# Writing down TensorE's order in the RWKV layer of a four-layer trunk

## The chip, the core and the metric

The kernel runs as one program on one core of a Trainium2 chip. The metric is the device time of one execution in microseconds (us). The engines are named as the profile names them: PE is TensorE (PEld its weight loads), DVE is VectorE, ACT is ScalarE, POOL is GpSimd, SP issues DMAs. Each engine works through its own queue in the order in which the compiled program put it there.

## The reference

A sequence of 1024 tokens and a context of 256 tokens, 1024 wide, go through four mixer layers: 0 and 3 are gated linear recurrences, 1 is an mLSTM, and layer 2 is the RWKV-7 mixer that this case is about. Cut to what matters, layer 2 is

```
xs = h + (shifted - h) * mu                     # six mixtures of h and its shift
r, k, v, z = xs[:4] @ w_rkvz                    # four projections, 1024 x 1024 each
decay, a = low-rank functions of xs[4], xs[5]
for t, forward and then again backward, per head of 64:
    s = s * decay_t - (s @ kk_t) (kk_t * a_t)^T + v_t k_t^T
    y_t = s @ r_t
out = (groupnorm(y) + bonus) * silu(z) @ w_out
x = x + gate * out
```

The context is scanned first, and its last states start the scan of the sequence, in both directions. All is float32 at the borders.

## The kernel before, in words

The 1280 tokens are five blocks of 256, the channels eight tiles `e` of 128 (two heads each). `rwkv_scan` does layer 2. Two kinds of work share the engines in it.

**The scan** runs in 40 batches. `batch(n)` gives a step `i` (0 to 4) and a tile `e`; tiles 0 to 3 run in batches 0 to 19, tiles 4 to 7 in batches 20 to 39. One batch is one block forward and one block backward of one tile, in four chunks of 64 tokens. It has four functions:
- `prep(n)` makes the chunk operands. For each direction two small matmuls (pA below: L1043, L1045) give decay and rate, ACT and DVE turn them into `AR` and `BK`, then sixteen matmuls of `AR` with `BK` (L1093, two halves of eight, pB below) fill PSUM banks `px`; ACT copies parts of them into `DG` (L1098, L1099), of which there is one buffer, and `RB`, and DVE masks the rest into `X` (L1102). Transposes of `BK` follow (L1111).
- `inverse(n)` inverts the triangular 64 x 64 blocks. DVE transposes `DG` into `LN` (L1147), does a forward substitution of 28 small instructions (L1164, L1165), transposes back (L1167) and transposes the 16 x 16 inverses into `E16` (L1171). Then TensorE doubles the block size twice, in four groups of 32 x 32 matmuls (L1177, L1182, L1189, L1195; i1 to i4 below), with ACT copies and DVE additions between them (L1184, L1185).
- `chain(n, step)` is one chunk of the recurrence: matmuls c1 (L1236), an ACT copy, c2 (L1240), ACT copies, c3 (L1246), four DVE updates of the state in `UZ` or `st`, and the output matmuls c4 (L1253, L1255).
- `finish(n)` is the group norm of a batch whose two directions are summed.

The loop over `n` issues, in this order: steps 2 and 3 of batch n-1 interleaved with steps 0 and 1 of batch n, `finish(n - 2)`, `inverse(n + 1)`, `prep(n + 2)`, and then projections.

**The projections** are the generators `group` and `output`. One pass is `project`: eight input tiles `xs`, eight times the three matmuls of `mm3` (L110 to L112; each float32 operand is a high and a low part) into a bank of `pz`, after which ACT or DVE empties the bank. `mixed` makes one input tile (ACT L861, DVE L81, ACT L881, POOL L86), `half` one half of a pass's weights (DMA, ACT L890, POOL L86), `kk_norm` normalizes a tile of keys with two more small matmuls (L982, L990). The value projection (L924 to L926) has tokens as the stationary operand. The list `fill` says in which batches which generator is pulled, and how often: 8 pulls in batches 0 to 1, 14 in 2 to 5, 10 in 6 to 9, 12 in 10 to 17, 12 in 18 to 25, 24 in 26 to 30, 24 in 31 to 36, 8 in 38 to 40.

What sets the order: the program is traced in the order above, and a scheduler then orders each engine's queue by its own model of the machine, with the trace's order as priority. `issue_after` keeps DVE's part of the projections of batch n behind the last DVE instruction of batch n-3. So the order in which projections and scan share TensorE is the scheduler's, not the source's.

Of the kernel before, what the change touches and what calls it, by code (L numbers as in the profile page):

```python
# [11 lines left out]
ALU = mybir.AluOpType  # L12
# [16 lines left out]
class Net:  # L29
# [756 lines left out]
    def rwkv_scan(self, es, hd, zd, yd, xd):  # L786
# [107 lines left out]
        def project(w_ap, xs, n):  # L894
            ps = bank(pz, "pz")[:, 0:n]
            for k in range(len(xs)):
                if k % 4 == 0:
                    w = half(w_ap[:, k * 128:k * 128 + 512])
                self.mm3(ps, w, k % 4, xs[k], (0, n), k == 0, k == len(xs) - 1)
            return ps  # L900

# [3 lines left out]

        def group(blks, what, wave=0):
            n = 256 * len(blks)
            for g in what:
                xs = [mixed(g, k, blks) for k in range(8)]
                if g >= 4:  # L910
                    ps = project(self.a["r7_l1"][g - 4], xs, n)
                    t = tile_("po", [128, 512], bufs=3)
                    S.activation(out=t[:, 0:n], in_=ps, func=AF.Tanh if g == 4 else AF.Copy)
                    out_blocks(blks, lambda b: ld[b][:, g - 4, :], t)
                    yield
                elif g == 2:
                    for i, b in enumerate(blks):
                        for q in (wave,):
                            acc = [bank(pz, "pz") for _ in range(2)]
                            for k in range(8):  # L920
                                w = half(self.a["r7_wv"][q][:, k * 512:k * 512 + 512])
                                for c in range(2):
                                    tk = slice(i * 256 + c * 128, i * 256 + c * 128 + 128)
                                    mm(acc[c], xs[k][0][:, tk], w[0], start=k == 0, stop=False)  # L924
                                    mm(acc[c], xs[k][0][:, tk], w[1], start=False, stop=False)
                                    mm(acc[c], xs[k][1][:, tk], w[0], start=False, stop=k == 7)  # L926
                                if k == 3:
                                    yield
                            for c in range(2):
                                t = tile_("po", [128, 512], bufs=3)  # L930
                                S.copy(out=t, in_=acc[c])
                                for j in (0, 1):
                                    nc.sync.dma_start(out=vd[b][8 * q:8 * q + 8, :, 2 * c + j, :].rearrange("h s v -> s h v"),
                                                      in_=t[hr[j]].rearrange("p (h v) -> p h v", h=8))
                            yield
                else:
                    for e in range(4 * wave, 4 * wave + 4):
                        ps = project(self.a["r7_w"][g, e], xs, n)
                        t = tile_("po", [128, 512], bufs=3)
                        if g == 3:  # L940
                            S.activation(out=t[:, 0:n], in_=ps, func=AF.Tanh, scale=0.5)
                            self.stt(V, t[:, 0:n], t[:, 0:n], 1.0, ps, ALU.add, ALU.mult)
                            out_blocks(blks, lambda b: zd[e][:, b * 256:(b + 1) * 256], t)
                        else:
                            S.copy(out=t[:, 0:n], in_=ps)
                            out_blocks(blks, lambda b: krk[b][e, :, 1 - g, :], t)
                        if g == 1:
                            kk_norm(e, t, n, blks)
                        yield

        def output(blks, ks, src):

            n = 256 * len(blks)
            xs = []
            for k in ks:
# [8 lines left out]
                xs.append((hi, lo))  # L964
            s = 0 if blks[0] else 1
            for e in range(8):
                t = tile_("po", [128, 512], bufs=3)
                for i, b in enumerate(blks):
                    nc.sync.dma_start(out=t[:, i * 256:(i + 1) * 256], in_=src[e][:, b * 256:(b + 1) * 256])
                ps = project(self.a["r7_w_out"][e][:, ks[0] * 128:], xs, n)  # L970
                self.stt(V, t[:, 0:n], ps, gate[:, e, s:s + 1], t[:, 0:n], ALU.mult, ALU.add)
                out_blocks(blks, lambda b: xd[e][:, b * 256:(b + 1) * 256], t)
                yield

        def kk_norm(e, kt, n, blks):

            sq = tile_("kq", [128, 512], bufs=1)
            S.activation(out=sq[:, 0:n], in_=kt[:, 0:n], func=AF.Square, scale=kk_v[:, e:e + 1])
            nt = n // 128
            ps = bank(pi, "pi")  # L980
# [7 lines left out]
            ps = bank(pi, "pi")  # L988
# [27 lines left out]
        def prep(n):  # L1016
# [16 lines left out]
            for d in (0, 1):  # L1033
# [10 lines left out]
                for o, w, j in oj:  # L1044
                    mm(o, w[r], lw[1][r, j, :], start=False, stop=j == 1)  # L1045
                sg = sgs[d]
# [30 lines left out]
                X = tile_("X%d" % d, [128, 4, 2, 128], bufs=3)  # L1077
# [224 lines left out]
        def run(*gens):  # L1302
            for g in gens:
                yield from g
# [207 lines left out]
```

## Time and profile before

| | us |
|---|---|
| median of 3 runs (4715.73 to 4727.37) | 4717.35 |
| the profiled execution's own time | 4715.13 |
| its span, first to last instruction | 4713.0 |
| PE busy, whole span (87%) | 4093.5 |
| DVE busy, whole span (70%) | 3313.9 |
| ACT busy, whole span (45%) | 2110.1 |
| POOL busy, whole span (48%) | 2271.5 |

The scan of layer 2 fills the span from about 2030 to about 4100 us. Busy is the share of time in which the engine ran at least one instruction. [...] "Idle before" in a group's row is the time that the engine stood still just before such an instruction, with what ended it.

### The profile page before, as it was taken

The numbers are of one execution on the slowest core, as the hardware profiler recorded it, in microseconds if no ns is written. First come the engines' busy times: TensorE is split into PE (matmuls) and PEld (weight loads), VectorE is DVE, ScalarE is ACT, GpSimd is POOL, SyncE is SP. The second block draws the span as 40 slices with busy tenths as digits, with TensorE's granted clock in tenths as the row PEclk, the third lists the DMA queues.
The fourth block names the chain that finished last, engine by engine and source line by source line (L and its number), as shares of the span: only waits on it lengthen the run. The fifth ranks groups of instructions, "written<-read, shape, count | busy, mean of one in ns | idle before, by whom it ended". The sixth has DMA issues, their size and how long they took to land. (4 is left out here: it accounts for less than half of the span.)

```text
span 4713.0 us, 84318 instructions
## 1 busy us (share of the span) xinstructions
PE 4093.5 (87%) x32068; PEld 3313.0 (70%) x32068; DVE 3313.9 (70%) x6218; ACT 2110.1 (45%) x4476; POOL 2271.5 (48%) x1989
## 2 busy tenths in 40 slices
PE   6999888999999989668988888888898888779988
PEld 3687768988889868445667666666666676557767
DVE  4478656545545533687988888988889889658875
ACT  3576322222222210645656545445566434256661
POOL 2466533333333331366666545555456654356662
PEclk9999989999999999768788777667588787689989
DMA  5311422222222342434444333223244443321122
GB/s 202 116 51 51 141 90 77 90 88 92 88 88 88 116 136 71 157 119 131 139 134 142 121 102 109 88 91 106 85 139 129 148 154 114 100 99 52 47 95 97
DMA packets 317749, 504.50 MB, mean 107 GB/s; under 512 B 55168, under 2 KB 201600, under 8 KB 317216
## 3 DMA queue, kind: packets, MB, share of 16 engines
q1 hardware_dynamic: 317344, 499.12, 33.1%
q8 instruction: 252, 4.13, 0.4%
q14 instruction: 153, 1.25, 0.1%
HBM read 406.02 MB, written 92.96 MB: 106 GB/s over the span
## 5 line engine op out<-in xcount | busy, mean ns | idle before, releaser
L86 POOL TENSOR_TENSOR wlo<-wraw,whi 128x512 fp32r<-128x512 f32 (+3 forms) x437 | 713.8, 1635 | 922.5 <-DVE whi L101 453.3
L112 PE MATMUL pm<-hhi,wlo 128*128 128x512 f32 (+1 forms) x1648 | 611.9, 374 | 32.1 <-POOL wlo L86 32.1
L111 PE MATMUL pm<-hlo,whi 128*128 128x512 f32 (+1 forms) x1648 | 620.1, 377 | 9.9 <-DVE hlo L81 9.9
L110 PE MATMUL pm<-hhi,whi 128*128 128x512 f32 (+1 forms) x1648 | 617.7, 375 | 0.6 <-ACT hhi L288 0.6
L101 DVE CAST whi<-wraw 128x1024 fp32r<-128x1024 f32 (+4 forms) x189 | 170.0, 900 | 336.5 <-PE pm L111 171.1
L86 POOL TENSOR_TENSOR xl<-mx,xh 128x512 fp32r<-128x512 f32 (+1 forms) x240 | 288.6, 1205 | 221.1 <-ACT xh L881 181.7
L110 PE MATMUL pz<-xh,whi 128*128 128x512 f32 (+1 forms) x784 | 333.8, 428 | 51.2 <-ACT whi L890 22.0
L112 PEld LDWEIGHTS pm<-hhi,wlo 128*128 128x128 f32 x1648 | 316.0, 192 | 87.2 <-POOL wlo L86 37.8
L111 PEld LDWEIGHTS pm<-hlo,whi 128*128 128x128 f32 x1648 | 316.0, 192 | 65.8 <-DVE hlo L81 11.4
L110 PEld LDWEIGHTS pm<-hhi,whi 128*128 128x128 f32 x1648 | 316.8, 192 | 53.8 <-issue 1.7
L111 PE MATMUL pz<-xl,whi 128*128 128x512 f32 (+1 forms) x784 | 330.1, 422 | 22.1 <-POOL xl L86 18.2
L110 PE MATMUL pm<-yhi,whi 128*128 128x512 f32 (+1 forms) x816 | 303.9, 377 | 44.5 <-DVE x L81 16.2
L112 PE MATMUL pz<-xh,wlo 128*128 128x512 f32 (+1 forms) x784 | 329.5, 421 | 6.7 <-POOL wlo L86 4.9
L111 PE MATMUL pm<-ylo,whi 128*128 128x512 f32 (+1 forms) x816 | 304.7, 374 | 3.9 <-POOL ylo L86 3.3
L112 PE MATMUL pm<-yhi,wlo 128*128 128x512 f32 (+1 forms) x816 | 297.9, 372 | 1.6 <-POOL wlo L86 1.6
L81 DVE SCALAR_TENSOR_TENSOR x<-pm,mod,x 128x512 f32<-128x512 f32 (+1 forms) x208 | 136.6, 665 | 184.3 <-PE pm L112 168.2
L1093 PE MATMUL px<-AR,BK 64*128 64x128 f32 x1280 | 204.3, 362 | 67.1 <-ACT BK L1071 37.6
L110 PEld LDWEIGHTS pz<-xh,whi 128*128 128x128 f32 x784 | 175.5, 225 | 94.9 <-ACT xh L881 28.2
L1093 PEld LDWEIGHTS px<-AR,BK 64*128 64x128 f32 x1280 | 171.9, 253 | 93.4 <-ACT BK L1071 46.1
L890 ACT CAST whi<-wraw 128x512 fp32r<-128x512 f32 x276 | 169.7, 617 | 142.5 <-PE pz L111 47.6
L81 DVE SCALAR_TENSOR_TENSOR mx<-hp,vecs,mx 128x256 f32<-128x256 f32 (+3 forms) x280 | 198.4, 731 | 46.3 <-ACT mx L861 45.5
L1164 DVE TENSOR_TENSOR ltmp<-LN 128x28 f32<-128x28 f32 (+6 forms) x560 | 219.0, 391 | 12.1
(356 smaller groups left out, 11041.3 us busy)
## 6 DMA issues: line engine op xcount, KB each, us to landing
wraw<-in_r_w SPq DMA_DIRECT2D x144, 256.0 KB, 3.1
kin<-r7krk SPq DMA_DIRECT2D x72, 384.0 KB, 3.3
mw<-in_mod_w SPq DMA_DIRECT2D x48, 512.0 KB, 6.9
mw<-in_mod_w SPq DMA_DIRECT2D x96, 256.0 KB, 2.6
wraw<-in_lru_w_in SPq DMA_DIRECT2D x40, 512.0 KB, 3.6
hp<-r7h SPq DMA_DIRECT2D x160, 128.0 KB, 2.2
wraw<-in_r_wv SPq DMA_DIRECT2D x80, 256.0 KB, 3.1
UZ<-r7v SPq DMA_DIRECT2D x160, 128.0 KB, 2.9
```

The source lines that it names most:

```text
L81: i = eng.scalar_tensor_tensor(out=out, in0=in0, scalar=scalar, in1=in1, op0=op0, op1=op1, **k)
L86: eng.tensor_tensor(out=out, in0=a, in1=b, op=op)
L101: nc.vector.tensor_copy(out=hi, in_=raw)
L110: mm(out, w[0][:, c], x[0][:, a:a + b], start=first, stop=False)
L111: mm(out, w[0][:, c], x[1][:, a:a + b], start=False, stop=False)
L112: mm(out, w[1][:, c], x[0][:, a:a + b], start=False, stop=last)
L890: S.copy(out=hi, in_=raw)
L1093: mm(pss[hh][:, c * 128:(c + 1) * 128], BK[r, c, 64 - 64 * hh:192 - 64 * hh], AR[r, c, :], start=True, stop=True)
L1164: V.tensor_tensor(out=tv, in0=c, in1=x, op=ALU.mult)
```

## The change: an order on TensorE

1. `group` and `output` no longer issue anything; they list passes. `rows` is a pass as before, cut into units of three matmuls (`mm3`); `cols` is the value projection, cut into units of six. `stream` walks the passes unit by unit, loads each half of the weights one half ahead, and makes the next pass's input tiles one by one during the last pass that uses the present ones. `kk_norm` is cut in three, runs its matmuls after units 2 and 5 of the next pass, and takes a bank of `pz` instead of `pi`.
2. `prep`, `inverse`, `chain` and `finish` become generators that yield where TensorE waits for another engine.
3. The time of a batch is a grid of 40 parts. `at` gives each piece of the scan its part; between two pieces `project` issues as many units as `rate` says: the projections of batches 6 to 37 now come from one stream at a constant 1488/32 = 46.5 matmuls of 512 columns per batch; batches 0 to 1 have (336 - 72)/2 = 132, batches 2 to 5 have 84.
4. At the end every TensorE instruction from `mark` on gets a dependency on the one before it (it orders the queue and adds no wait), so TensorE's order is the one written. The other engines' orders are still the scheduler's.

Matmuls, casts, vector instructions and DMAs are the same in kind; DVE has 5948 instructions in both programs.

```diff
+        def rows(job, w_ap, done):
+            n, ks = job.n, len(job.tiles)
+            hs = [w_ap[:, k * 128:k * 128 + 512] for k in range(0, ks, 4)]
+            def steps():
+                ps = bank(pz, "pz")[:, 0:n]
+                for k in range(ks):
+                    yield lambda w: self.mm3(ps, w, k % 4, job.xs[k], (0, n), k == 0, k == ks - 1)
+                done(ps)
+            return job, hs, 4, steps, 3 * n / 512
+        def stream(passes):
...
+            for pi_, (job, h, per, steps, cost) in enumerate(passes):
+                nxt = passes[pi_ + 1][0] if pi_ + 1 < len(passes) else job
...
+                for k, step in enumerate(steps()):
+                    if k % per == 0:
+                        if k:
+                            ready.pop(0)
+                        if len(ready) < 2:
+                            ahead()
+                    step(ready[0])
+                    if late and k in (2, 5):
+                        next(late[0], None)
...
+                    if nxt is not job:
+                        nxt.make()
+                    yield cost
...
-            ps = bank(pi, "pi")
+            ps = bank(pz, "pz")
...
+        INV = (10, 26, 28, 31, 33, 35, 36)
...
+        def project(amount):
+            nonlocal debt
+            debt += amount
+            while debt > 0:
+                with self.tc.issue_after(order_after[-3]) if len(order_after) >= 3 else ExitStack():
+                    c = next(dense, None)
+                if c is None:
+                    break
+                debt -= c
+        preps = {0: prep(0), 1: prep(1)}
+        drain(preps[0])
+        project(36)
+        drain(inverse(0))
+        project(36)
...
         for n in range(41):
-            for step in (0, 1):
-                if n:
-                    chain(n - 1, step + 2)
-                if n < 40:
-                    chain(n, step)
-            if n > 1:
-                finish(n - 2)
-            if n < 39:
-                inverse(n + 1)
-            if n < 38:
-                prep(n + 2)
+            dense, a, z, total = next(f for f in fill if f[1] <= n < f[2])
+            rate = (total - 72 * (a == 0)) / (z - a) / 40
...
+            for c, step, t in ((n - 1, 2, 0), (n - 1, 3, 16), (n, 0, 10), (n, 1, 26)):
+                if 0 <= c < 40:
+                    gens.append(at(chain(c, step), (t, t + 4, t + 8, t + 12, t + 14)))
+            if n < 39:
+                gens.append(at(preps[n + 1], (1, 5, 9, 11, 12)))
+                gens.append(at(inverse(n + 1), INV))
+            if n < 38:
+                preps[n + 2] = at(prep(n + 2), (13, 17, 19))
             if n > 1:
+                gens.append(at(finish(n - 2), (3, 21, 23)))
+            t0 = 0
+            for t, _, g in sorted(events, key=lambda v: v[:2]):
+                if t > t0:
+                    project(rate * (t - t0))
+                    t0 = t
+                next(g, None)
+            project(rate * (40 - t0))
...
+        last = None
+        for i in nc.cur_bb.bb.instructions[mark:]:
+            if str(i.engine).split(".")[-1] == "PE":
+                if last is not None:
+                    self.tc.add_manual_dep(i, last.name, mybir.DependencyInfo(mybir.DependencyClass.NoSync, mybir.DependencyReason.DATA), reason="order")
+                last = i
```

The order on TensorE before, where the inverse of batch 15 begins: the two halves of pB (L1093) of the next batch stand ahead of i1 (L1177).

```order
L1236 MATMUL pc<-UZ,X_26512 64x64
L1093 MATMUL px<-AR,BK 128x128 x4
L1236 MATMUL pc<-UZ,X_26512 64x64
L1236 MATMUL pc<-UZ,X_26545 64x64
L1093 MATMUL px<-AR,BK 128x128 x4
L1240 MATMUL pc<-U_27265,DT_16453 64x64 x3
L1177 MATMUL pi<-E_26886,DO 32x32 x32
L1111 MATMUL px<-ident,BK 128x64 x8
```

So the next batch's `DG` could be filled while this batch's i1 still waited. The order on TensorE in the change, at i1 (now L1241) of a batch in the constant part of the stream; c4 is now L1325 and L1327, i2 L1247.

```order
L1241 MATMUL pi<-E_35147,DO 32x32 x32
L110 MATMUL pz<-xh,whi 128x512
L111 MATMUL pz<-xl,whi 128x512
L112 MATMUL pz<-xh,wlo 128x512
L1325 MATMUL pc<-UZ,X_33796 64x64 x2
L1325 MATMUL pc<-UZ,X_33871 64x64 x2
L1327 MATMUL pc<-UZ,RB_33799 64x64 x2
L1327 MATMUL pc<-UZ,RB_33874 64x64 x2
L1247 MATMUL pi<-D_35146,QQ 32x32 x32
```

A unit of the projections and a piece of the scan alternate. Further on in the same queue, 24 rows after that i2, both halves of the next batch's pB (now L1153) come, behind i1 to i4:

```order
L1305 MATMUL pc<-UZ,X_34432 64x64 x2
L1305 MATMUL pc<-UZ,X_34466 64x64 x2
L1153 MATMUL px<-AR,BK 128x128 x8
L110 MATMUL pz<-xh,whi 128x512
L111 MATMUL pz<-xl,whi 128x512
L112 MATMUL pz<-xh,wlo 128x512
L1310 MATMUL pc<-U_35586,DT_16451 64x64 x4
L1153 MATMUL px<-AR,BK 128x128 x8
```

In the change pB of the next batch stands behind i1 in every batch.

## Rows read from the trace of the kernel before

**Rows 1.** The page: granted clock by fortieths of the span, in tenths.

```profile
PEclk9999989999999999768788777667588787689989
```

**Rows 2.** Busy time by stretch; columns stand in the header row.

```profile
core 0: us, PE busy (x) PEld busy (x) DVE busy (x) ACT busy (x) POOL busy (x), PEclk, DMA share, GB/s
2500.00:4000.00 1500.00, 1270.94 (x15124) 1001.48 (x15122) 1307.54 (x2824) 774.24 (x2090) 826.47 (x888) 0.75 0.39 117
```

**Rows 3.** VectorE's groups, 2100 to 4100: busy, mean ns, idle before.

```profile
L1102 DVE TENSOR_TENSOR X<-px,mk 64x512 f32<-64x512 f32 x152 | 104.4, 687 | 55.2 <-ACT RB L1101 52.0
L81 DVE SCALAR_TENSOR_TENSOR UZ<-UZ,W,pc 64x64 f32<-64x64 f32 x480 | 133.4, 278 | 31.7 <-PE pc L1246 20.3 <-ACT DT L1200 0.3
```

**Rows 4.** TensorE's groups, same stretch.

```profile
L1236 PE MATMUL pc<-UZ,X 128*64 128x64 f32 x1272 | 143.2, 281 | 55.8 <-DVE UZ L81 50.4 <-DMA mx<-y 2.8 <-DVE y L1258 1.8
L1177 PE MATMUL pi<-E,DO 32*32 32x32 f32 x2560 | 40.0, 208 | 17.9 <-DVE E L1171 13.1 <-DVE kq L81 4.8
L110 PE MATMUL pz<-xh,whi 128*128 128x512 f32 (+1 forms) x680 | 289.5, 428 | 18.4 <-ACT xh L881 9.8 <-ACT whi L890 2.8 <-DVE po L81 2.6
```

**Rows 5.** Timeline, VectorE: the LN transposes of batches 0, 6, 38 (start, us).

```profile
2026.12 2.07 DVE L1147 STREAM_TRANSPOSE LN<-DG 128x1024 f32<-128x1024 f32 x1 [2.95 <-ACT DG L1099]
2407.01 1.99 DVE L1147 STREAM_TRANSPOSE LN<-DG 128x1024 f32<-128x1024 f32 x1
3990.75 1.99 DVE L1147 STREAM_TRANSPOSE LN<-DG 128x1024 f32<-128x1024 f32 x1 [0.62 <-ACT DG L1099]
```

**Rows 6.** Timeline, batch 15 to 16: E16, pB, i1, LN.

```profile
2918.48 0.43 DVE L1171 STREAM_TRANSPOSE E<-D 128x256 f32<-128x256 f32 x1
2922.79 1.16 PE L1093 MATMUL px<-AR,BK 64*128 64x128 f32 x8
2924.25 0.75 PE L1177 MATMUL pi<-E,DO 32*32 32x32 f32 x64
2925.05 2.04 DVE L1147 STREAM_TRANSPOSE LN<-DG 128x1024 f32<-128x1024 f32 x1
```

**Rows 7.** Timeline, batch 26 to 27: E16, pB, c4, i1, c4, i2, pB, LN.

```profile
3429.57 0.44 DVE L1171 STREAM_TRANSPOSE E<-D 128x256 f32<-128x256 f32 x1
3429.64 1.16 PE L1093 MATMUL px<-AR,BK 64*128 64x128 f32 x16
3431.66 0.45 PE L1255 MATMUL pc<-UZ,RB 64*64 64x64 f32 x8
3432.41 0.75 PE L1177 MATMUL pi<-E,DO 32*32 32x32 f32 x64
3439.62 0.69 PE L1255 MATMUL pc<-UZ,RB 64*64 64x64 f32 x8
3440.24 1.07 PE L1182 MATMUL pi<-D,QQ 32*32 32x32 f32 x64
3441.25 2.08 PE L1093 MATMUL px<-AR,BK 64*128 64x128 f32 x16
3445.38 2.12 DVE L1147 STREAM_TRANSPOSE LN<-DG 128x1024 f32<-128x1024 f32 x1
```

**Rows 8.** Timeline, TensorE: projections at clock 0.5 and at 1.0.

```profile
2245.93 0.63 PE L925 MATMUL pz<-wlo,xh 128*128 128x512 f32 x1
2246.35 0.63 PE L926 MATMUL pz<-whi,xl 128*128 128x512 f32 x1
2272.61 0.39 PE L111 MATMUL pz<-xl,whi 128*128 128x512 f32 x1
2272.84 0.39 PE L112 MATMUL pz<-xh,wlo 128*128 128x512 f32 x1
```

**Rows 9.** Projection tiles alone, two stretches: busy, count, clock of the stretch.

```profile
3300.00:3400.00 100.00, 10.63 (x31) 7.21 (x29) 0.00 (x0) 1.17 (x2) 0.52 0.30 89
3400.00:3500.00 100.00, 49.02 (x188) 34.95 (x189) 4.37 (x8) 3.90 (x8) 0.81 0.43 128
```

**Rows 10.** Timeline, TensorE: i1 of batch 0.

```profile
2124.25 0.75 PE L1177 MATMUL pi<-E,DO 32*32 32x32 f32 x64
```

More of the change, by code (lines that the diff above doesn't have):

```diff
@@ L892, in half @@
             return hi, lo
[L894 to L900, printed above, removed]
         def out_blocks(blks, dst, t):
@@ new lines, in cols, with steps, mms @@
+        def cols(job, i, w_ap, done):
+            def steps():
+                acc = [bank(pz, "pz") for _ in range(2)]
+                for k in range(8):
+                    def mms(w):
+                        for c in range(2):
+                            tk = slice(i * 256 + c * 128, i * 256 + c * 128 + 128)
+                            mm(acc[c], job.xs[k][0][:, tk], w[0], start=k == 0, stop=False)
+                            mm(acc[c], job.xs[k][0][:, tk], w[1], start=False, stop=False)
+                            mm(acc[c], job.xs[k][1][:, tk], w[0], start=False, stop=k == 7)
+                    yield mms
+                for c in range(2):
+                    done(c, acc[c])
+            return job, [w_ap[:, k * 512:k * 512 + 512] for k in range(8)], 1, steps, 6
@@ new lines, in stream, with ahead @@
+        def stream(passes):
+            passes = list(passes)
+            hs = [ap for _, h, *_ in passes for ap in h]
+            ready = []
+            nh = 0
+            def ahead():
+                nonlocal nh
+                if nh < len(hs):
+                    ready.append(half(hs[nh]))
+                    nh += 1
+            for pi_, (job, h, per, steps, cost) in enumerate(passes):
+                nxt = passes[pi_ + 1][0] if pi_ + 1 < len(passes) else job
+                while len(job.xs) < len(job.tiles):
+                    job.make()
+                if not ready:
+                    ahead()
[4 more added lines that the diff above has]
+                        if len(ready) < 2:
+                            ahead()
+                    step(ready[0])
+                    if late and k in (2, 5):
+                        next(late[0], None)
+                        if k == 5:
+                            late.pop()
+                    if nxt is not job:
+                        nxt.make()
+                    yield cost
+                ready.pop(0)
+            drain(*late)
@@ L908, in group, with done @@
             for g in what:
-                xs = [mixed(g, k, blks) for k in range(8)]
+                job = Job(blks, [lambda g=g, k=k: mixed(g, k, blks) for k in range(8)])
                 if g >= 4:
[L911 to L915, printed above, removed]
+                    def done(ps, g=g):
+                        t = tile_("po", [128, 512], bufs=3)
+                        S.activation(out=t[:, 0:n], in_=ps, func=AF.Tanh if g == 4 else AF.Copy)
+                        out_blocks(blks, lambda b: ld[b][:, g - 4, :], t)
+                    yield rows(job, self.a["r7_l1"][g - 4], done)
@@ L916, in group @@
                 elif g == 2:
                     for i, b in enumerate(blks):
[L918 to L935, printed above, removed]
@@ L1298, in finish, with drain @@
                     mm(ps[r, c * 64:(c + 1) * 64], y[r, c, :], self.ident[r, r], start=True, stop=True)
+            yield
             S.activation(out=yo[:, 0:64 * m], in_=ps[:, 0:64 * m], func=AF.Identity, scale=0.5, bias=hlb[:, e:e + 1])
             out_blocks(blks, lambda blk: yd[e][:, blk * 256:(blk + 1) * 256], yo)
-        def run(*gens):
+        def drain(*gens):
             for g in gens:
-                yield from g
-        def pull(it, n):
-            for _ in range(n):
-                if next(it, 0) == 0:
-                    return
+                for _ in g:
+                    pass
         early = True
@@ L1384, in rwkv_scan @@
-        finish(39)
+        both = lambda *gens: (p for g in gens for p in g)
+        fill = [(stream(group(G1, (4, 5) + krv)), 0, 2, 336), (stream(group(G2, (4, 5) + krv)), 2, 6, 336),
+                (stream(both(*(group(g, krv, 1) for g in (G0, G1, G2)), *(group(g, (3,), w) for g in (G0, G1, G2) for w in (0, 1)),
+                             output(G0, range(8), self.xsrc), output(G1, range(4), self.xsrc), output(G2, range(4), self.xsrc))), 6, 38, 1488),
+                (stream(output(G2, range(4, 8), xd)), 38, 41, 96)]
```

127 lines of the change are left out of this document (77 added, 50 removed).

## The prediction, on record before the change was timed

> **What bounds the kernel now.** I read the page first, then busy time by stretch, then the groups of VectorE (DVE) and TensorE (PE) inside layer 2, then the timeline of single batches. The page shows a clock that is high at both ends and between 0.5 and 0.8 over most of the scan [rows 1]. From 2500 to 4000 us PE is busy 1271 of 1500 us and DVE 1308 of 1500 us, with a mean clock of 0.75 [rows 2]: neither is full, each waits for the other in turn. VectorE stands still before masking `X` (55.2 us in all, for ACT's copies out of pB) and before the state updates (31.7 us) [rows 3]; TensorE stands still before c1 (55.8 us, for those updates), before i1 (17.9 us, for `E16`) and little before projections (18.4 us) [rows 4]. All these groups are of 2100 to 4100 us.
>
> A batch is measured from one LN transpose to the next. Batch 0 has it at 2026.1, batch 6 at 2407.0, batch 38 at 3990.8 [rows 5]. So the first six batches take 380.9 us and the other 32 take (3990.8 - 2407.0)/32 = 49.5 us each. DVE is busy 1307.5/1500 of that, 43.1 us; 6.4 us per batch are its gaps and waits. That is the most that an order can win there.
>
> Two sections of a batch matter. A is DVE's way from LN to `E16`; B is from `E16` to the next LN. In the order before, pB of the next batch may stand ahead of i1, and the trace shows what that is worth: pB ran at 2922.8, i1 only at 2924.3, and the next LN followed 6.1 us after the end of `E16` [rows 6]. Where pB stands behind i1 and i2, the same section took 3445.4 - 3430.0 = 15.4 us [rows 7]. Counted along TensorE's order before, pB is wholly ahead of i1 in 20 of 39 batches; in the change in none.
>
> **The change part by part.** *Even projections.* Matmuls are the same in number, so this is worth what the clock and the waits make of it. Neighbouring projections of 512 columns start 0.42 us apart at clock 0.5 and 0.23 us apart at 1.0 [rows 8]; a stretch with 31 of them ran at 0.52, the next with 188 at 0.81 [rows 9]. The change gives every batch from 6 to 37 46.5, some 94 per 100 us, and I expect a clock like the mean of these two, no gain by itself. Waits of projections for weights and inputs (18.4 us before the first of three matmuls [rows 4]) lie on TensorE, which has time to spare in section A; loading one half ahead and making inputs one by one I cost at nothing, hidden there; between 0 and -18 us.
>
> *A serial loop per batch.* In the change i1, i2, i3, i4 stand ahead of the next batch's pB, which fills the only `DG`, which LN reads. So a batch lasts A plus the longer of B, DVE's own work there, and L, TensorE's way from i1 through pB. With every DVE instruction at the mean duration of its kind, DVE's order before has 38.6 us in A and 10.5 us in B (means of batches 6 to 37); in the change 30.3 and 18.0. Neighbours overlap, so these sums stand for 43.1 us of busy time: a factor of 0.89. In the change A is then 27.0 us, and I leave 1.7 us of waits in it, near the 55.2/40 = 1.4 us per batch that `X` shows [rows 3]. For L the order lists i1 to i4, two c4, one c1, two c2, one c3, two halves of pB and 21 projections. At clock 1.0: four times 0.75, four times 0.45 for c4 (two groups each), four times 0.45, twice 1.16, 21 times 0.23, which is 13.7 us. At the low clock: four times 1.07, eight times 0.69, twice 2.08, 21 times 0.42, which is 22.8 us [rows 7, 8]. From pB's end to LN it took 3445.4 - 3443.3 = 2.1 us [rows 7]. The steps of ACT and DVE between i1 and i4 that the units in between don't cover I put at 2 us; the trace doesn't show them in this order, and 15.4 us [rows 7] is the lower end for L, 22.8 + 4 = 27 us the upper. I take 18 us, near the full clock, since TensorE's work in L is dense. DVE's own B is unlike from batch to batch; in 21 of 32 it is below 20 us after the factor. The mean of the longer of B and 18 us is 20.4 us. A batch: 28.7 + 20.4 = 49.1 us, against 49.5: 32 x 0.4 = **13 us less**. What is late next is DVE in section A, with i1 behind it.
>
> *The first six batches.* DVE's order gives A 207 us and B 148 us in sum there. A: 207 x 0.89 + 6 x 1.7 = 195 us; B, with L of 20 to 26 us as more projections stand in it: 157 us. Together 352 us against 380.9: **29 us less**. This goes where i1 of batch 0 stood till 2124.3 [rows 10], 98 us behind its LN, with a long run of projections ahead of it; in the change 36 matmuls stand there.
>
> *The start.* Ahead of the first LN DVE's order has 84 us of work before and 74 us now (fewer input tiles come first): 10 x 0.89, **9 us less**; 0 if a DMA is late.
>
> *Small edits.* `kk_norm` on a bank of `pz`, its matmuls later: nothing, since two projection banks alternate and its results are needed batches later; if both banks were held, some 2 us for each of twenty calls. The yields and the dependency issue nothing. No DMA is added; the order of SP follows the stream, and inputs are asked for 8 units ahead.
>
> Sum: 13 + 29 + 9 = 51 us off the profiled execution's 4715.1, which is 2.2 us below the median of the runs: **4664 us**. About 0.3%, 14 us, is what a measurement here can tell from no change.
>
> **The rivals.** *The loop at the low clock (slower).* TensorE waits at i1 in every batch: in section A it has some 15 us of work in 28.7 us. [...] Rows: 31 projections in 100 us, clock 0.52 [rows 9]. With L = 22 us the longer of B and L is 23 us, a batch lasts 51.7 us: 32 x 2.2 = 70 us more, less some 20 at the start: 4765 us. With 27 us it is 27.3, a batch 56 us: 208 us more, the first six batches 53 us more, 9 saved: 4967 us. From L = 20 us on it eats the 38 us of the first batches. For it: the mean clock of 0.75 [rows 2]; against it: in L the units are close together. [...]
>
> *VectorE alone (much faster).* If pB's data came early enough, or ACT and DVE needed no time between i1 and i4, L would be about 13 us and hidden; a batch would be 43.1 us of DVE work and 2 us of waits. 32 x 4.4 = 141 us and 38 us at the start: 4536 us. For it: waits before c1 (55.8 us [rows 4]) should vanish, since c3 and the next c1 are 8 parts of 40 apart. Against it: the order shown, pB behind i1.
>
> *Nothing (same).* What DVE stops waiting for at c1 it waits for at LN: 4715 us. That the change doesn't do what it says can nearly be left out: TensorE's order is the one shown; but the queues of ACT, DVE and POOL are still the scheduler's, so their due times may not be the grid's.
>
> **How the numbers follow.** Forecast 0.40, much faster 0.15, same 0.14, slower 0.31 (most of it near 4765). So faster by over 0.3%: 0.55, within: 0.14, slower: 0.31. The range of 8 in 10 reaches from 4550, nearly all of the forecast's way to VectorE alone, to 4800, past the first price of the slower rival; left out are the far ends of both. The forecast's own range is 4600 to 4700.
>
> **What would show it.** In the changed profile, from 2500 to 3900 us, right is: LN to LN near 49 us; TensorE's idle time before i1 grown from 17.9 us to 100 or more; that before c1 well below 55.8 us; VectorE's waits before `X` and LN, for ACT, grown; L from E16 to LN near 18 us in batches where B is short; i1 of batch 0 within 70 us of its LN. A clock under 0.7 there with L above 20 us speaks for the slower rival; LN to LN of 45 us with DVE busy over 93% for the much faster one. If TensorE does not wait at i1 at all, the loop that the forecast rests on is wrong.

## The result, and the profile after

The changed kernel takes 5029.5 us (median of four runs, 5024.7 to 5032.4) against 4716.5 (4704.5 to 4727.4): a ratio of 1.066, with a 95% interval of 1.064 to 1.069. It is **313 us slower**; 51 us faster were forecast, and the range ended at 4800. The profiled execution has a span of 5030.7 us (before 4713.0).

Where the 317.7 us came from shows along the LN transposes. The timeline after, with the LN of batches 0, 6, 24 and 38, answers to [rows 5], and i1 of batch 0 to [rows 10]:

```profile
1997.60 1.99 DVE L1210 STREAM_TRANSPOSE LN<-DG 128x1024 f32<-128x1024 f32 x1
2464.39 2.07 DVE L1210 STREAM_TRANSPOSE LN<-DG 128x1024 f32<-128x1024 f32 x1
3510.31 1.95 DVE L1210 STREAM_TRANSPOSE LN<-DG 128x1024 f32<-128x1024 f32 x1
4287.11 1.91 DVE L1210 STREAM_TRANSPOSE LN<-DG 128x1024 f32<-128x1024 f32 x1
2038.00 0.75 PE L1241 MATMUL pi<-E,DO 32*32 32x32 f32 x64
```

- Before the first LN: 1997.6 against 2026.1, 28.5 us less.
- Batches 0 to 5: 466.8 against 380.9 us, 85.9 more.
- Batches 6 to 37: 1822.7 against 1583.7 us, 239.0 more. A batch takes **57.0 us in place of 49.5**.
- From the LN of batch 38 to the end: 743.6 against 722.3 us, 21.3 more.

The stretch of [rows 2], after (same columns), and the page's granted clock, which answers to [rows 1]:

```profile
2500.00:4000.00 1500.00, 1055.82 (x12717) 788.37 (x12714) 1083.84 (x2378) 674.90 (x1820) 688.37 (x754) 0.72 0.30 94
```

```profile
PEclk9999989999999996787877677676777767779989
```

TensorE's clock is given as a share of its full speed: each of its 190 entries in the trace before and 294 in the trace after is 0.5, called the low clock below, or 1.0; a value between is a mean over a stretch. Busy time fell from 1271 to 1056 us on TensorE and from 1308 to 1084 us on VectorE: both wait more, and the clock is 0.72 in place of 0.75. (VectorE ran 6218 instructions in both traces; the 5948 given above the prediction is not what they count.) Whom the engines wait for is in the groups from 2100 to 4100 us (busy, mean ns, idle before), for VectorE's masks and state updates as in [rows 3], for c1, i1 and the projections as in [rows 4]:

```profile
L1163 DVE TENSOR_TENSOR X<-px,mk 64x512 f32<-64x512 f32 x132 | 90.8, 688 | 152.6 <-ACT RB L1162 141.4 <-PE pz L112 7.2 <-PE pz L111 2.1
L81 DVE SCALAR_TENSOR_TENSOR UZ<-UZ,W,pc 64x64 f32<-64x64 f32 x400 | 111.3, 278 | 93.0 <-PE pc L1317 72.6 <-ACT whi L890 6.9 <-ACT xh L881 6.2
L1305 PE MATMUL pc<-UZ,X 128*64 128x64 f32 x1064 | 73.9, 274 | 0.0
L1241 PE MATMUL pi<-E,DO 32*32 32x32 f32 x2176 | 33.0, 223 | 155.9 <-DVE E L1234 155.8
L110 PE MATMUL pz<-xh,whi 128*128 128x512 f32 (+1 forms) x566 | 305.3, 539 | 4.7 <-DVE kq L81 3.3 <-ACT po L986 1.2
```

The wait before c1 (55.8 us) is gone and that before the projections is down from 18.4 to 4.7 us, as forecast. In their place TensorE waits 155.9 us for `E16` before i1 (17.9 before), and VectorE nearly three times as long before `X` and before `UZ`. The two engines take turns, as one batch shows, that of the LN at 3510.31 (timeline; TensorE's i1 to i4 and pB, VectorE's `E16`, masks and next LN, one of ACT's copies):

```profile
3541.40 0.43 DVE L1234 STREAM_TRANSPOSE E<-D 128x256 f32<-128x256 f32 x1
3541.88 1.08 PE L1241 MATMUL pi<-E,DO 32*32 32x32 f32 x64 [4.31 <-DVE E L1234]
3545.72 0.94 PE L1247 MATMUL pi<-D,QQ 32*32 32x32 f32 x64
3549.99 1.06 PE L1255 MATMUL pi<-E,OF 32*32 32x32 f32 x32 [2.07 <-DVE s L1362]
3552.56 1.06 PE L1262 MATMUL pi<-D,QP 32*32 32x32 f32 x32
3558.85 1.16 PE L1153 MATMUL px<-AR,BK 64*128 64x128 f32 x16
3560.74 0.36 ACT L1162 COPY RB<-px 64x256 f32<-64x256 f32 x1
3561.13 0.69 DVE L1163 TENSOR_TENSOR X<-px,mk 64x512 f32<-64x512 f32 x1 [0.95 <-ACT RB L1162]
3561.88 0.48 PE L1153 MATMUL px<-AR,BK 64*128 64x128 f32 x2 [0.58 <-DVE X L1163]
3562.95 1.79 PE L1153 MATMUL px<-AR,BK 64*128 64x128 f32 x14 [0.59 <-DVE X L1163]
3565.45 0.69 DVE L1163 TENSOR_TENSOR X<-px,mk 64x512 f32<-64x512 f32 x1 [2.56 <-ACT RB L1162]
3566.18 2.00 DVE L1210 STREAM_TRANSPOSE LN<-DG 128x1024 f32<-128x1024 f32 x1
```

`E16` ends at 3541.8 and the next LN starts at 3566.2: section B is 24.4 us, all of it TensorE's way L. Seen from the right end: LN stands behind the last mask, which waits for ACT's copies out of the second half of pB; that half waits for the banks of the first, which the masks hold till 3562.9; the first half starts 5.2 us after the end of i4, behind projections and c steps; and i1 to i4 take 11.7 us with their steps on ACT and VectorE.

### The profile page after: what moved, and what is told of

Read it like the earlier page. It is cut to its first block, busy times and chain, and to the rows that moved or that the text cites. A ratio compares the mean times of both kernels' runs of the same rounds, so it can differ in the third digit from the quotient of the medians.

```text
span 5030.7 us, 84260 instructions
## 1 busy us (share of the span) xinstructions
PE 4055.4 (81%) x32068; PEld 3228.4 (64%) x32068; DVE 3289.1 (65%) x6218; ACT 2111.2 (42%) x4476; POOL 2257.6 (45%) x1989
## 5 line engine op out<-in xcount | busy, mean ns | idle before, releaser
L110 PE MATMUL pz<-xh,whi 128*128 128x512 f32 (+1 forms) x784 | 417.4, 532 | 34.2 <-DMA hp<-r7h 19.0
L111 PE MATMUL pz<-xl,whi 128*128 128x512 f32 (+1 forms) x784 | 346.4, 442 | 5.9 <-POOL xl L86 5.5
L112 PE MATMUL pz<-xh,wlo 128*128 128x512 f32 (+1 forms) x784 | 341.9, 436 | 4.3 <-POOL wlo L86 2.3
L110 PEld LDWEIGHTS pz<-xh,whi 128*128 128x128 f32 x784 | 188.0, 240 | 92.4 <-ACT whi L890 23.7
L1163 DVE TENSOR_TENSOR X<-px,mk 64x512 f32<-64x512 f32 x160 | 110.1, 688 | 174.9 <-ACT RB L1162 163.2
L112 PEld LDWEIGHTS pz<-xh,wlo 128*128 128x128 f32 x784 | 196.8, 251 | 38.9 <-POOL wlo L86 4.6
L111 PEld LDWEIGHTS pz<-xl,whi 128*128 128x128 f32 x784 | 198.3, 253 | 18.3 <-POOL xl L86 11.1
```

The lines of the kernel that those rows point to most:

```text
L110: mm(out, w[0][:, c], x[0][:, a:a + b], start=first, stop=False)
L111: mm(out, w[0][:, c], x[1][:, a:a + b], start=False, stop=False)
L112: mm(out, w[1][:, c], x[0][:, a:a + b], start=False, stop=last)
L1163: V.tensor_tensor(out=X[o, :, hh, :], in0=p3[o], in1=mk[d][o].unsqueeze(1).to_broadcast([64, 4, 128]), op=ALU.mult)
```

## The experiments

Lines left out of an edit are marked with three dots. In the table a batch is the mean from LN to LN over batches 6 to 37; VectorE's busy share and the clock are of 2500 to 4000 us. Ratios are to the kernel before on the same chip, with 95% intervals.

| run | us | ratio (interval) | batch, us | DVE | clock |
|---|---|---|---|---|---|
| before | 4716.5 | 1 | 49.5 | 87% | 0.75 |
| after | 5029.5 | 1.066 (1.064 to 1.069) | 57.0 | 72% | 0.72 |
| e5_pb_behind | 4993.9 | 1.060 (1.058 to 1.061) | 56.1 | 74% | 0.68 |
| e15_one_dep | 5019.0 | 1.065 (1.063 to 1.067) | 57.4 | 73% | 0.68 |
| e2_noorder | 4703.0 | 0.998 (0.996 to 1.000) | 48.6 | 89% | 0.76 |
| e6_even | 4712.2 | 0.999 (0.998 to 1.001) | 48.8 | 90% | 0.76 |
| e13_proj_free | 5037.0 | 1.069 (1.067 to 1.071) | 56.6 | 74% | 0.71 |
| e14_pb_free | 4827.0 | 1.024 (1.023 to 1.026) | 51.6 | 85% | 0.75 |
| e1_decouple | 4820.4 | 1.023 (1.022 to 1.025) | 50.9 | 84% | 0.75 |
| e8_decouple_noorder | 4698.3 | 0.997 (0.995 to 0.998) | 48.9 | 90% | 0.76 |
| e9_decouple_pr | 4861.9 | 1.031 (1.028 to 1.033) | 51.8 | 82% | 0.76 |
| e11_pb_first | 4966.8 | 1.053 (1.051 to 1.054) | 55.6 | 77% | 0.74 |
| e12_pb_first_noorder | 4714.3 | 1.000 (0.998 to 1.001) | 49.4 | 89% | 0.76 |
| e10_pb_next | 4941.8 | 1.048 (1.046 to 1.050) | 54.7 | 79% | 0.72 |
| e3_noproj | 5111.6 | 1.084 (1.081 to 1.086) | 57.9 | 75% | 0.70 |
| e7_dummy | 5022.2 | 1.066 (1.063 to 1.069) | 57.3 | 72% | 0.78 |
| e16_mask_first | 5029.9 | 1.066 (1.063 to 1.070) | 57.3 | 72% | 0.72 |
| e17_e8_mask | 4659.7 | 0.989 (0.986 to 0.991) | 48.0 | 90% | 0.77 |
| e18_e2_mask | 4718.8 | 1.000 (0.999 to 1.001) | 48.7 | 88% | 0.76 |

### Which part of the change costs the time

**One dependency in the kernel before.** pB of the next batch stands behind i4:

```diff
...
+                if n - 1 in ends:
...
+                    self.tc.add_manual_dep(first, ends[n - 1].name, ...)
...
```

> The kernel before with one dependency in each batch: the first matmul of pB of the next batch stands behind the last of i4 on TensorE; the scheduler orders all else. Theory 1 (the loop): a batch has A of 30 us or more and then L, so 53 to 58 us in place of 49.5 and 4830 to 4990 us in all; the sections without projections stay. Theory 2 (even, thin projections) and theory 3 (a written order of everything): no projection moves to another batch and the order stays the scheduler's, so within 30 us of 4716.

4994 us and 56.1 us a batch: theory 1, a little above its range. No projection and no other order was touched by hand.

**The changed kernel without its written order.** The last loop, which ties each TensorE instruction to the one before, is left out:

```diff
...
-                if last is not None:
-                    self.tc.add_manual_dep(i, last.name, ...)
...
```

> The changed kernel without the last loop, which ties each TensorE instruction to the one before: the scheduler orders TensorE again, all else stays (projections by threes, grid as order of the program, even rate). Theory 1 (the loop): the scheduler can put pB ahead of i1 where E16 is late, as it did before in 20 of 39 batches, so near the kernel before: 4680 to 4780 us. Theory 2 (even, thin projections): 4950 us or more. Theory 3 (a written order as such): 4680 to 4780 us too.

4703 us. So units of three matmuls, the even rate, the stages and the grid as program order cost nothing; theories 1 and 3 are left. In this trace pB of the next batch is wholly ahead of i1 in 17 of 39 batches and half ahead in 17 more (20 and 11 in the kernel before, none in the changed one).

**Even projections alone**, in the kernel before: the groups of batches 6 to 36 in one stream.

```diff
...
+                (run(*(group(g, krv, 1) for g in (G0, G1, G2)), ..., output(G2, range(4), self.xsrc)), 82, 6, 38),
```

> The kernel before with its projections of batches 6 to 37 spread evenly over them (82 units in one stream), each unit whole and placed by the scheduler. Theory 1 (the loop): the order of pB and i1 stays the scheduler's, so within 40 us of 4716. Theory 2 (even spreading holds the clock low and stretches the loop): 4850 to 5000 us, with a clock under 0.75 from 2500 to 4000 us.

4712 us: no effect. With the run before it, theory 2 is out.

**The same dependency in place of the written order**, in the changed kernel (the edit of the first run on the second):

> The changed kernel without the last loop (4703 us so), with one dependency per batch in its place: the first matmul of pB of the next batch stands behind the last of i4. If this one constraint is enough for the loss: 4950 to 5060 us and batches of 55 to 58 us, as the same dependency in the kernel before gave 4994. If it takes the whole written order: below 4850 us.

5019 us, within 11 us of the changed kernel. **One constraint is enough for the whole loss.** From 2500 to 4000 us, and VectorE's groups from 2100 to 4100 us:

```profile
2500.00:4000.00 1500.00, 1165.01 (x12452) 907.46 (x12448) 1091.08 (x2360) 678.88 (x1803) 705.41 (x759) 0.68 0.33 99
```

```profile
L1168 DVE TENSOR_TENSOR X<-px,mk 64x512 f32<-64x512 f32 x132 | 90.8, 688 | 190.8 <-ACT RB L1167 186.6 <-PE pz L112 2.2 <-PE pz L110 0.8
```

VectorE is as idle as in the changed kernel, and at the same place.

**The written order without the projections**, which the scheduler places:

```diff
...
+            free.update(i.name for i in nc.cur_bb.bb.instructions[mark:])
...
-            if str(i.engine).split(".")[-1] == "PE":
+            if str(i.engine).split(".")[-1] == "PE" and i.name not in free:
```

> The changed kernel with its written order for the scan's instructions alone; the scheduler places the projections and the steps of kk_norm. If the order of the scan is the loss: 4950 to 5080 us. If the places of the projections, by threes between the steps, are: 4700 to 4800 us.

5037 us: giving the projections' places back to the scheduler wins nothing. (A grid that moved them by hand, further down, lost 82 us.)

**The written order without pB** (the same edit around pB's matmuls):

> The changed kernel with its written order for every TensorE instruction but those of pB, which the scheduler places; it puts the first half ahead of i1 and the second between i2 and i3. If the loop is the loss: most of it goes, 4650 to 4800 us. If the other waits of the written order cost as much (as the run with pB ahead of i1 by the grid would say): 4850 to 4980 us.

4827 us, between the two. 203 us of the 313 come back with pB; the other 110 stay. TensorE's waits from 2100 to 4100 us, for the steps that the order still holds:

```profile
L1328 PE MATMUL pc<-UZ,X 128*64 128x64 f32 x1168 | 80.8, 273 | 101.1 <-DVE UZ L81 94.4 <-DVE st L81 6.5
L1265 PE MATMUL pi<-D,QP 32*32 32x32 f32 x1184 | 36.0, 227 | 54.2 <-ACT QP L1262 54.2
L1196 PE MATMUL px<-rkb,tp 128*128 128x2 f32 x112 | 22.0, 301 | 85.3 <-POOL tp L86 81.0 <-ACT BT L1178 4.3
L1244 PE MATMUL pi<-E,DO 32*32 32x32 f32 x2368 | 32.0, 209 | 14.6 <-DVE E L1237 14.6
```

The wait before i1 is down to 14.6 us, and c4, i4 and the bonus matmuls of `tp` hold TensorE up: an order that cannot be left when its next instruction is not ready. That this is the 110 us is not shown. On the chip pB is wholly ahead of i1 in 1 of 39 batches and half ahead in 10, so part of the loop is still there: from i1 to LN it takes 15.0 us, and i1 comes 11.3 us after `E16` (means of batches 6 to 37). The two parts were not separated.

### Other grids

**i1 to i4 behind pB of the next batch.**

```diff
...
+            for c, step, t in ((n - 1, 2, 5), (n - 1, 3, 20), (n, 0, 17), (n, 1, 31)):
...
+                at(n, inverse(n + 1), (17, 46, 48, 51, 53, 55, 56))
...
-            for c, step, t in ((n - 1, 2, 0), (n - 1, 3, 16), (n, 0, 10), (n, 1, 26)):
...
-                gens.append(at(inverse(n + 1), INV))
...
```

The loads of `UZ` are also issued earlier, ahead of i1, here and in every other run of this section.

> The changed kernel with one part of its grid moved: i1 to i4 of a batch stand behind pB of the next batch (parts 6 to 16 of the next forty, in place of 26 to 36), the four state steps 4 to 7 parts later; projections, their even rate and the fixed order of TensorE stay. Theory 1 (the loop i1, pB, LN, E16, i1 is what costs): a batch falls from 57.0 us to between 45 and 49 us, so 32 x 8 to 32 x 12 = 256 to 384 us less than the changed kernel's 5030, 4650 to 4775 us; TensorE's idle time before i1 falls from 156 us to under 40. Theory 2 (the even, thin projections hold the clock low and that stretches everything): 4970 us or more, as the rate is the same. Theory 3 (a written order of TensorE as such makes it wait): 4900 us or more.

4820 us: 209 us better, but short of 4775, the end of theory 1's range. TensorE's wait before i1 is 0 from 2100 to 4100 us, under 40 as theory 1 had it, but a batch fell to 50.9 us, not to 45 to 49. Without its written order:

> As the run with i1 to i4 behind pB of the next batch, and without the last loop, so that the scheduler orders TensorE by the new grid as program order. If the written order as such costs what kept that run at 50.9 us a batch (waits before pR for POOL, before i3 for DVE): a batch falls to 46 to 48.5 us and the time to 4640 to 4720 us. If the new place of i1 to i4 costs it (they come a whole half batch later, so that the state steps wait for them): 4780 us or more.

4698 us, 122 us less: leaving the written order out gives back the rest, though a batch at 48.9 us is just above the 46 to 48.5 expected. With the bonus matmuls (pR) later in the written order:

> As the run with i1 to i4 behind pB of the next batch, with one step later in its fixed order: the small matmuls of tp (pR, for the bonus) stand at part 24 in place of 11, behind two more steps. If waits of a fixed order are what is left there: the 67 us of TensorE's idle time before pR go, and 30 to 70 us of the time, to 4750 to 4790 us. If VectorE or the loop sets the batch anyway: within 15 us of 4820.

4862 us, 41 us worse: a miss. The wait that was to go did not go. TensorE's waits before pR from 2100 to 4100 us, first with i1 to i4 behind pB alone, then with pR later too:

```profile
L1193 PE MATMUL px<-rkb,tp 128*128 128x2 f32 x120 | 29.3, 348 | 74.5 <-POOL tp L86 67.1 <-ACT BT L1175 7.3
L1194 PE MATMUL px<-rkb,tp 128*128 128x2 f32 x112 | 21.7, 298 | 85.0 <-POOL tp L86 85.0
```

The waits before c4 (58.2 to 88.2 us) and i4 (27.2 to 52.0 us) grew as well. So the run does not tell what that wait is worth; it shows that a step put later by hand is not sure to wait less.

**pB ahead of i1.** The state steps run one after the other, so that pB can stand at parts 17 and 20:

```diff
...
-        INV = (10, 26, 28, 31, 33, 35, 36)
+        INV = (3, 26, 28, 31, 33, 35, 36)
...
-            for c, step, t in ((n - 1, 2, 0), (n - 1, 3, 16), (n, 0, 10), (n, 1, 26)):
+            for c, step, t in ((n, 0, 0), (n - 1, 3, 2), (n, 1, 14), (n, 2, 28)):
...
-                preps[n + 2] = at(prep(n + 2), (13, 17, 19))
+                gens.append(at(prep(n + 2), (4, 8, 10, 17, 20, 23, 25, 27)))
...
```

> The changed kernel with a grid in which pB of the next batch stands ahead of i1 (parts 17 and 20 against 26), made possible by running the four state steps of a batch one after the other from part 0 (0, 14, 28, 42 in place of 10, 26, 40, 56), so that the X buffers come free; fixed order and even projections stay. If the loop through pB is the cause: a batch is set by VectorE's 43 us and some waits, 45 to 49 us, so 4600 to 4750 us in all, and DVE is busy 85% or more from 2500 to 3900 us. If a fixed order or even, thin projections cost it: 4850 us or more.

> As the run with pB ahead of i1 by the grid, without the last loop, so that the scheduler orders TensorE. If waits in a fixed order are a cost of their own beside the loop: 20 to 100 us faster than that run, and 4600 to 4700 us. If not: within 15 us of it.

4967 us with the order and 4714 without. For theory 1 alone the first is a plain miss; the second is 253 us faster, far more than the 20 to 100 expected, and still above 4700. The groups of 2100 to 4100 us, with the order:

```profile
L1153 PE MATMUL px<-AR,BK 64*128 64x128 f32 x1104 | 135.9, 380 | 135.7 <-DVE X L1163 72.6 <-ACT BK L1131 60.4 <-DVE X L86 1.9
L1247 PE MATMUL pi<-E,DO 32*32 32x32 f32 x2176 | 32.8, 222 | 0.0
L81 DVE SCALAR_TENSOR_TENSOR UZ<-UZ,W,pc 64x64 f32<-64x64 f32 x412 | 114.9, 279 | 105.4 <-PE pc L1316 85.3 <-ACT xh L881 7.7 <-ACT whi L890 3.6
```

The wait before i1 is 0, so the loop through `E16` is gone. TensorE now waits 135.7 us before pB for `X` and `BK`, and VectorE 85.3 us for c3, of which one stands two parts behind pB in TensorE's order. That looks like another loop of two queues; it is read from the waits and was not tested. In all three grids the scheduler's order of TensorE gives 4698 to 4714 us and a written one 4820 to 5030 us. That VectorE's order, still the scheduler's, fits none of the written ones is the likely reason; a kernel with both orders written was not tried.

### What sets the size of the loop

**pB right behind i4** (parts 34 and 37, still behind i1 to i4):

```diff
...
-                gens.append(at(preps[n + 1], (1, 5, 9, 11, 12)))
+                gens.append(at(preps[n + 1], (1, 11, 12)))
...
-                preps[n + 2] = at(prep(n + 2), (13, 17, 19))
+                preps[n + 2] = at(prep(n + 2), (13, 17, 19, 34, 37))
```

> The changed kernel with pB of the next batch moved up to stand right behind i4 (parts 34 and 37 in place of 41 and 45), still behind i1 to i4; projections, even rate and fixed order stay. If TensorE's way from i1 to pB sets the batch, whatever stands in it: the 7.2 us that the changed kernel shows from i4 to pB fall to 2 or 3, a batch falls by 4 to 6 us, and the time by 130 to 230 us (38 batches), to 4800 to 4900. If VectorE's own work in that section (some 18 us busy) sets it, or the batch is 57 us for another reason: within 40 us of 5030.

4942 us: 88 us better, between the two ranges expected. From the start of i4 to pB it fell from 7.2 to 2.3 us, but i1 came 9.2 us after `E16` in place of 4.5: the work of the order ahead of i1 is then late in its place, likely the projections that left the gap.

**Fewer projections in the loop**: none in parts 26 to 40 and 0 to 5.

```diff
+            amount = lambda t: min(max(t - 5, 0), 21) * 40 / 21
...
-                    project(rate * (t - t0))
+                    project(rate * (amount(t) - amount(t0)))
...
```

> The changed kernel with no projection in parts 26 to 40 and 0 to 5 of a batch, and nearly twice as many in parts 5 to 26; the rest of the grid and the fixed order stay. If the work in L (from i1 to pB) sets the batch: 12 to 15 projections fewer there, at 0.23 to 0.42 us, so 3 to 6 us less in each of 38 batches, and the time falls by 100 to 230 us to 4800 to 4930 us; the section from LN to E16 has idle time of TensorE enough for them. If it is the steps of ACT and DVE between i1 and i4 that set L, and the projections only fill them: within 30 us of the changed kernel's 5030.

5112 us, 82 us worse: a miss for both. From i1 to the end of pB it took 20.9 us (23.7 in the changed kernel), but at a mean granted clock of 0.60 in place of 0.76; and i1 came 7.7 us after `E16` in place of 4.5.

**Matmuls of constants ahead of i1**, in the bank that i1 overwrites:

```diff
+            for _ in range(4):
+                mm(ps.rearrange("p u t -> p (u t)"), mk[0], lng.rearrange("p e v -> p (e v)"), start=True, stop=True)
+                yield
...
-        INV = (10, 26, 28, 31, 33, 35, 36)
+        INV = (10, 16, 19, 22, 24, 26, 28, 31, 33, 35, 36)
```

> The changed kernel with four matmuls of constants (128x512, float32) before i1 of each batch, spread over its wait for E16, in the bank that i1 overwrites; the output does not use them. If L is long because TensorE waits ahead of it and so starts it at the low clock: the mean clock from i1 to pB rises from 0.76 to 0.9 or more, L falls from 23.7 to below 20 us, and the time falls by 100 us or more, to below 4930. If the clock is not what makes L: within 30 us of 5030, or up to 100 us above it, by the time that the matmuls take.

5022 us. From 2500 to 4000 us, and TensorE's wait before i1 from 2100 to 4100 us:

```profile
2500.00:4000.00 1500.00, 1111.86 (x12840) 786.68 (x12839) 1082.21 (x2378) 677.11 (x1819) 685.43 (x756) 0.78 0.31 94
```

```profile
L1244 PE MATMUL pi<-E,DO 32*32 32x32 f32 x2176 | 29.0, 207 | 74.6 <-DVE E L1234 64.1 <-DVE s L1359 10.5
```

The matmuls filled half of the wait (74.6 us left of 155.9), and the clock of the stretch rose from 0.72 to 0.78. i1 now starts at the full clock in 23 of the 32 batches 6 to 37, where it did in 11. But from i1 to the end of pB the mean clock rose only from 0.76 to 0.78, and that section stayed at 23.4 us (23.7 before). So more batches start i1 at the full clock with the idle time filled, and the time did not follow: the low clock at the start of i1 is not what makes L long. What L would be at the full clock all the way, no run shows.

**The masks of `X` ahead of ACT's copies.** One line moved:

```diff
...
+                    V.tensor_tensor(out=X[o, :, hh, :], in0=p3[o], ...)
                     S.copy(out=DG[b0, u, :], in_=p3[b0, :, 0:32])
                     ...
                     S.copy(out=RB[r], in_=p3[r, :, 64:128])
-                    V.tensor_tensor(out=X[o, :, hh, :], in0=p3[o], ...)
```

> The changed kernel with one line moved: VectorE's mask of X stands ahead of ACT's four copies out of the same bank of pB, in place of behind them. If VectorE's idle time there is a term of the loop (152.6 us before X from 2100 to 4100 us, 4.6 us a batch): 80 to 170 us faster, 4860 to 4950. If it is only the place where VectorE stands while TensorE's way and ACT's copies set the next LN: within 40 us of 5030, as the copies then start 0.7 us later and VectorE waits for DG in place of RB.

5029.9 us: nothing. The groups of 2100 to 4100 us show the wait moved, not gone:

```profile
L1159 DVE TENSOR_TENSOR X<-px,mk 64x512 f32<-64x512 f32 x132 | 90.9, 689 | 134.5 <-PE px L1153 131.8
L1210 DVE STREAM_TRANSPOSE LN<-DG 128x1024 f32<-128x1024 f32 x34 | 68.6, 2016 | 15.9 <-ACT DG L1161 15.3
```

VectorE now waits there for pB itself, and for ACT at LN. Idle time before an instruction names the place, not the price.

**The same line in the two grids without a written order.**

> The run with i1 to i4 behind pB and no written order (4698 us), with the mask of X ahead of ACT's copies. VectorE is busy 90% there and waits little before X: if that wait is real, 10 to 30 us faster, 4670 to 4690; if not, within 10 us.

> The changed kernel without the written order (4703 us), with the mask of X ahead of ACT's copies: it waits 29.7 us before X from 2100 to 4100 us. If that wait is real, 10 to 30 us faster; if it moves to LN, within 10 us.

4660 us, the fastest run of all, 1.2% below the kernel before (interval 0.9 to 1.4%) and faster than either range expected, and 4719 us. One edit made 39 us less in one grid; in the other nothing that stands clear of noise (ratios 0.998 and 1.000, with intervals that overlap). The scheduler makes another order of the whole each time, so the gain can't be put down to the mask: it may belong to that order as found.

## Why the prediction was wrong

**The mechanism was right.** The forecast's second step, a serial loop of A and the longer of B and L because pB stands behind i1 to i4, is what the two runs with one dependency show to be enough for the loss. The signs named came too: TensorE waits 155.9 us before i1 (100 or more were named), VectorE's waits before `X` grew, the wait before c1 is gone, and i1 of batch 0 is 40.4 us behind its LN (within 70).

**Its size was wrong: the failed step is "I take 18 us, near the full clock" for L, with i1 taken to start as `E16` ends.** Means over batches 6 to 37, from the starts and ends of these instructions in the trace:

| section, us | forecast | after | e15_one_dep |
|---|---|---|---|
| A, LN to the end of `E16` | 28.7 | 26.6 | 36.8 |
| end of `E16` to i1 | 0 | 4.5 | 1.0 |
| start of i1 to start of i4 | | 10.4 | |
| start of i4 to pB | | 7.2 | |
| pB, first start to last end | | 6.1 | |
| i1 to the end of pB | | 23.7 | 18.3 |
| end of pB to LN | 2.1 | 2.1 | 1.3 |
| B, `E16` to LN | 20.4 | 30.3 | 20.6 |

L, from i1 to LN, is 25.8 us where 18 were taken: inside the bounds of 15.4 and 27, near the upper. The forecast's terms against the same sections of the trace:

| term of L, us | forecast | after |
|---|---|---|
| TensorE busy, i1 to the end of pB | 13.7 at clock 1.0 (22.8 at 0.5) | 19.0 at a mean of 0.76 |
| TensorE idle between i1 and i4 | 2 | 3.1 |
| TensorE idle from i4 to the end of pB | 0 | 1.6 |
| end of pB to LN | 2.1 | 2.1 |

By these terms L is 8.0 us longer (25.8 against 17.8). The largest part, 5.3 us by this count, is that L did not run near the full clock. The argument for it, "TensorE's work in L is dense", did not hold: TensorE is busy in 19.0 of 23.7 us, and the clock is 0.76. In the two batches with a clock over 0.9 it was busy 16.0 us there, in the seven under 0.7 21.8 us. The rest are waits between the steps: for `E32` and `QP` between i1 and i4, and before pB's second half, whose banks the masks of the first still hold. Beside L, i1 does not start as `E16` ends: in 15 of the 32 batches TensorE is over 2 us late there (4.5 us in the mean of all). In those 15 it is busy for 8.0 of the 9.6 us: the order's other work stands ahead of i1. A came out 2.1 us shorter than forecast.

Two smaller slips did not decide it. The row that gave the lower bound of 15.4 us [rows 7] has only half of pB behind i1 and i2, and i4 starts at 3450.7 there, after the next LN, so it says little of an L with all of them. And the factor of 0.89 is 43.1/48.3, from the order of the change; from the order before, to which the 43.1 us belong, it is 43.1/49.1 = 0.88. That makes A 0.4 us shorter per batch.

Seen from VectorE it is simpler. Its gaps of over 0.2 us, summed per batch, grew from 5.0 to 13.7 us, 12.7 of them in B; its work, the batch less the gaps, stayed near 44 us (49.5 - 5.0 and 57.0 - 13.7). The run with one dependency has 13.8 us of gaps although its L, 19.6 us from i1 to LN, and its B, 20.6 us, came out near the forecast: A there is 36.8 us, with 35.0 us of VectorE's work in it, and 7.1 us were left to fill B. So the forecast's other weak point is A at 28.7 us *together with* VectorE's work of B: the order can hold both only if that work is ready while pB is on its way.

**The rivals.** The loop at the low clock gave 56 us for a batch and 4967 in all; 57.0 and 5030 came. Its price was near, its reason half right: the clock in L, 0.76 in the mean, is the larger part of what the forecast missed, and i1 starts at the low clock in 21 of the 32 batches. But more starts at the full clock did not shorten the way from i1 to the end of pB (23.4 us against 23.7, e7_dummy), so it is not the start that makes it. "VectorE alone" asked for pB earlier; a written grid that brought it earlier did not get there either (4967 us). "Nothing" is what even projections came to, as the first step said.

**The first batches and the start.** 9 us less were forecast for the start, and 28.5 came; but 29 us less were forecast for the first six batches, and 85.9 us more came. The step counted VectorE's work and an L of 20 to 26 us; the means there are 33.4 us for A and 44.4 us for B, in which i1 comes 7.5 us late and L takes 36.9 us. Without the written order (e2_noorder) the same six took 428 us, 47 above the kernel before, and the first LN came nearly as early, at 2004.7: projections that no longer stand ahead of batch 0 stand inside the next ones, which is the likely reason. What a start gains by putting work off has to be counted where the work goes.

**The chances.** Slower had 0.31, most of it near 4765. From the break-even at L = 20 us, with bounds of 15.4 and 27, more than half of the interval lay on the slow side; the forecast's 18 was its estimate of L at the full clock all the way (13.7 + 2 + 2.1).

## What to carry to other kernels

Before writing an engine's order by hand, follow each loop that the order closes through the other engines, and price it with the waits in it, bank by bank, and at the clock that the trace shows for such a stretch (0.76 from i1 to the end of pB here), not with the matmuls at full speed. A written order on one engine against a scheduler's order on another can cost on its own (leaving it out gave back 122 and 253 us in the two other grids here): test it by leaving the order out and keeping the rest. And a wait that a moved line makes vanish may only change its name: look at the time from one batch to the next.

## What the runs showed of the hardware that was not expected

VectorE's mask of `X` starts when ACT's copy of `RB` ends (3560.74 + 0.36 us, mask at 3561.13), though the two read different halves of the partitions of one bank. The wait follows the order of the program's lines: with the mask moved ahead of the copies (e16_mask_first), the mask waits for pB (131.8 us from 2100 to 4100 us) where it waited for the copy (141.4 us), and ACT's first copy waits for the mask instead (60.8 us). No run here shows the two reads at the same time, so whether they could run so is not shown.

With part of i1's idle time filled, the granted clock of the stretch rose from 0.72 to 0.78 and the time stayed (5022 against 5030 us); with the projections moved out of the loop, the clock from i1 to pB fell from 0.76 to 0.60 and the time grew by 82 us. A higher mean clock was worth nothing where the added work lay in a wait.
